# Seven half-size products for eight in two branch projections of a hybrid decoder layer

## The chip, the core and the metric

The kernel runs on one core of a Trainium2 chip. The core has five engines, each with its own instruction queue that it works off in order: TensorE (PE, matrix products; its weight loads, PEld, overlap them), VectorE (DVE), ScalarE (ACT), GpSimd (POOL) and SyncE (SP, which here only starts transfers). ACT and POOL start transfers too. Matrix products write to PSUM, which has eight banks of 128 x 512 floats; everything else lies in SBUF or, when it does not fit, in DRAM.

The metric is the time of one execution on the device, in microseconds (us); less is better. Before the change it is 1789.28 us, the median of three runs from 1788.69 to 1789.63.

## The reference

One layer of a decoder trunk, for 1024 positions of width 1024 (biases, lesser gains and the second half cut here):

```python
h = rms_norm(x, norm1_g)
proj = h @ w_in                          # all projections, the last 3 x 1024 columns are gate logits
p_rwkv, p_sb, q_mem, gate_logits = split(proj)
y_a = rwkv7_branch(p_rwkv)               # recurrence over positions, branch 0, width 512
y_b = stick_breaking_branch(p_sb)        # causal attention, branch 1, width 512
y_m = memory_branch(q_mem, mem)          # attention into 256 memory tokens, branch 2, width 512
ys = stack([y_a, y_b, y_m], axis=2)
branch_out = einsum('btnc,ncd->btnd', ys, w_branch)
merged = sum(sigmoid(gate_logits) * branch_out, axis=2)
x = x + merged @ w_out
x = x + conv_ffn(rms_norm(x, norm2_g))
```

The change concerns the products `ys[n] @ w_branch[n]` (1024 x 512 by 512 x 1024) of branches 1 and 2, and where the gates (`sigmoid`, 24 blocks of 128 columns by 1024 positions) are computed.

## The kernel before

**Precision.** Every product is made of three: both operands are split into a high part (an ACT copy that rounds, `split_raw`, L83) and a low part (the raw value less the high one, on POOL at L89 or DVE), and `mm3` (L107) adds high x high, high x low, low x high in one PSUM bank. So each operand costs one ACT and one POOL or DVE operation, and each block of the product three matmuls per 128 rows of depth and 512 columns.

**Items and filler.** The work that only fills PE is a list of generators (`items`, L1983 to L2007), and one step of a generator is six matmuls of 512 columns. `stream` starts each one an item ahead, which starts its weight load. `weave` (L1953) puts them between the steps of a main stream that is full of waits; a ratio says how many filler steps go to one step of the main stream.

**The main stream beside the change** is `stage2` (L601): the recurrence in 16 chunks of three steps. In step A PE applies the state, and DVE copies the result (L656); in step B PE solves within the chunk, and ACT copies the result (L664); in step C PE makes the output and the new state, which DVE adds to the old one (L674), while ACT copies the output (L676). The next A needs the new state, and the banks from which the output was copied. Between them `norm_part` (L693) takes the group norm of finished chunks: sums on DVE (L699), squares on ACT (L706, four of them a step), the square root on POOL (L195), the rescaling on DVE (L715). Then `group_norm` (L718) turns the result on PE, multiplies and adds on DVE (L729, L730) and splits it (L734, L735) for branch 0's product in `branch_last` (L1317), which follows at once.

**The filler beside it**, from the mark "y1" on: branch 1's products, the load and split of branch 2's input, branch 2's products with four of its gates between them, and the last two gates of branch 0. A branch is eight `branch_item`s (L1277), one for each 128 columns of output, of four steps each: with the split weight and the split input it fills two banks, and DVE multiplies them by the gate (L1297). For branch 2 POOL then adds branch 1's result, read back from DRAM (L1299), and POOL stores the sum in `mrd` (L1300). Gates are computed by `gate_item` (L879): eight steps, two ACT copies out of PSUM (L885), a rescaling on DVE by `rbc` (L886), a sigmoid on ACT (L889), and a store to `gsd`, from which the products load them (L1283). Four gates of branch 2 are not stored but kept.

**Buffers.** Gates and results use the three buffers of tag "w4"; raw weights two ("wr"), split weights two and two ("wh", "wl"). The normalised input x lies split in 16 tiles (xhi, xlo, eight each) until the last gate is done.

**Order.** Instructions marked by `pinned` (L124) stay in program order on their engine; while `strict` is set, as in this stretch, each one is also tied behind the pinned one before it. All others, DMAs among them, are placed by a planner.

Of the kernel before, what the change touches and what calls it, by code (L numbers as in the profile page):

```python
# [12 lines left out]
F32 = mybir.dt.float32  # L13
# [37 lines left out]
class Trunk:  # L51
# [11 lines left out]
    def t4(self, tag="w4", dt=F32, n=1024):  # L63
        pool = self.pool_a if tag in ("A", "it") else self.pool_w
        return pool.tile([128, n], dt, name=self.nm(tag), tag=tag, bufs=self.bufs_w[tag])

# [130 lines left out]
    def startup(self):  # L197
# [9 lines left out]
        self.xhi, self.xlo = ([self.pool_x.tile([128, 1024], F32R, name=f"x{n}{k}") for k in range(8)] for n in ("hi", "lo"))  # L207
# [112 lines left out]
    def row_norm(self, sq):  # L320
# [11 lines left out]
        self.rbc = self.pool_x.tile([128, 1024], F32, name="rbc")  # L332
# [920 lines left out]
    def load_y(self, b, st):  # L1253
        nc = self.nc
        ys, out = [], []
        st["y"] = out

        def first():
            for k in range(4):
                ys.append(self.t4("A", F32R))  # L1260
                nc.sync.dma_start(ys[k].bitcast(F32), self.yd[b, k])

        def split(k):
            if k == 0:
                st["hi"] = self.pool_a.tile([128, 4, 1024], F32R, name=self.nm("yhi"), tag="inst")
            hi, y = st["hi"][:, k], ys[k]
            self.pinned(nc.scalar.activation(hi, y.bitcast(F32), AF.Copy))
            self.pinned(nc.vector.tensor_tensor(y, y.bitcast(F32), hi.bitcast(F32), ALU.subtract))
            out.append((hi, y))

        return first, {3 + k: functools.partial(split, k) for k in range(4)}

# [4 lines left out]
    def branch_item(self, b, d, st, first):  # L1277
        nc = self.nc
        if d % 2 == 0:
            st["w", d // 2] = self.split_w(self.I["w_br"][b, d // 2])  # L1280
        if (b, d) in self.stored:
            st["g", d] = self.t4()
            nc.sync.dma_start(st["g", d], self.gsd[b, d])  # L1283
        if not first:
            o = self.t4()
            nc.sync.dma_start(o, self.mrd[d])
        yield
        pp = [self.ps("mm"), self.ps("mm")]
        for k in range(4):
            self.branch_mm(d, st["w", d // 2], st["y"], pp, k)  # L1290
            if k == 1:
                self.close_gates()
            yield
        g = st.pop(("g", d))
        for h in range(2):
            hs = slice(h * 512, (h + 1) * 512)
            self.pinned(nc.vector.tensor_tensor(g[:, hs], pp[h], g[:, hs], ALU.mult))  # L1297
        if not first:
            (nc.vector if d == 7 else nc.gpsimd).tensor_tensor(g, g, o, ALU.add)  # L1299
        nc.gpsimd.dma_start(self.mrd[d], g)  # L1300

    def branch(self, b, first):
        st = {}
        load, hooks = self.load_y(b, st)
        items = []
        for d in range(8):
            if (b, d) not in self.stored:
                items.append(self.gate_item(b, d, keep=st))
            items.append(self.branch_item(b, d, st, first))
        return load, items, hooks  # L1310
# [654 lines left out]
    def run(self):  # L1965
# [8 lines left out]
        self.stored, self.open_gates = set(), []  # L1974
# [17 lines left out]
        self.stored = set(gq)  # L1992
# [12 lines left out]
        ld1, br1, sp1 = self.branch(1, True)  # L2005
        ld2, br2, sp2 = self.branch(2, False)
# [34 lines left out]
        next(st2)  # L2041
        need("y1")
        self.strict = True
        self.weave(st2, pump, 2.08, 0)
        self.weave(self.group_norm(), pump, 1.0, 0)
        self.strict = False
        drain(pump)
# [80 lines left out]
```

## Time and profile before

| | |
|---|---|
| median of three runs | 1789.28 us |
| the profiled execution | 1788.33 us, its span 1786.6 us |
| PE busy | 1774.7 us, 99% |
| DVE, ACT, POOL busy | 1185.1, 883.3, 698.3 us |
| stage 2 in the span | 785.00 to about 981 us |
| group norm's turn and the last gate | about 981 to 1016 us |
| clock granted to PE | 1.00 |

The profile is of one execution. A row of a timeline gives start, length, engine, line, operation, output<-input and shape, and how often; in brackets the idle time of the engine before it and what ended it. A row of the groups gives line, engine, operation, tiles, shapes and count, then busy us and mean ns of one, then the idle time before them by what ended it. "x2" in a timeline row is two instructions merged.

### The profile page before, as it was taken

What the parts mean: (1) busy time and instruction counts of PE and PEld (TensorE: products, weight loads), DVE (VectorE), ACT (ScalarE), POOL (GpSimd) and SP (SyncE); (2) the same over time, 40 slices, a digit from 0 to 9 for tenths busy, and PEclk for the clock granted to TensorE, in tenths of its full rate; (3) what the DMA queues carried; (4) which work ended last, traced back from release to release, by engine and by line L of the source; (5) the groups of instructions that cost most, each with busy time, mean ns of one, the idle gap of its engine ahead of it and who ended that gap; (6) DMA issues with size and microseconds to landing.
All of it is one profiled execution on the core that took longest, in us unless ns stands there. A gap on an engine that the chain in (4) does not pass through costs nothing.

```text
span 1786.6 us, 27452 instructions
## 1 busy us (share of the span) xinstructions
PE 1774.7 (99%) x10481; PEld 1442.4 (81%) x10481; DVE 1185.1 (66%) x1687; ACT 883.3 (49%) x1667; POOL 698.3 (39%) x409
## 2 busy tenths in 40 slices
PE   9999999999999999999999999999999999999999
PEld 7777778878888888787777888887888888888887
DVE  5666674787888655243533873698767777795597
ACT  6544344566566635444546434454444445445343
POOL 1233252222231012122433321257777677535454
PEclk9999999999999999999999999999999999999999
DMA  4256574111112333658763653323323333396475
GB/s 185 74 166 193 181 244 148 51 57 42 54 57 77 103 126 93 203 181 278 269 228 145 230 211 105 108 89 124 101 89 104 115 104 113 109 329 224 142 246 202
DMA packets 120757, 263.39 MB, mean 147 GB/s; under 512 B 28329, under 2 KB 41129, under 8 KB 120498
## 3 DMA queue, kind: packets, MB, share of 16 engines
q1 hardware_dynamic: 82434, 193.31, 33.1%
q10 hardware_dynamic: 34416, 55.72, 8.5%
q0 software_dynamic: 3776, 12.62, 2.3%
q8 instruction: 82, 1.34, 0.3%
q14 instruction: 49, 0.40, 0.1%
HBM read 180.04 MB, written 81.53 MB: 146 GB/s over the span
## 4 chain that ended last, share of the span: by engine, by line
PE 61%; issue 1%; DVE 1%; POOL 1%; ACT 1%; DMA 1%; ACTq 0%; DVEq 0%; POOLq 0%; SPq 0%
PE mm L139 53%; PE g L139 8%; PE g L122 1%; POOL dw L1854 1%; DMA vmd<-w 0%; ACT wh L83 0%; DMA qk<-vd 0%; DVE qk L715 0%; ACT w L885 0%; DVE gall L1646 0%; DVE w L886 0%; DVE ga L1635 0%; DVE keep L1874 0%; DVE g L1629 0%; DVE g L1630 0%
## 5 line engine op out<-in xcount | busy, mean ns | idle before, releaser
L89 POOL TENSOR_TENSOR wl<-wr,wh 128x1024 fp32r<-128x1024 f32 x58 | 147.8, 2550 | 368.2 <-ACT wh L83 355.0
L139 PE MATMUL mm<-xhi,wh 128*128 128x512 f32 x784 | 260.5, 413 | 1.4 <-ACT xhi L222 1.0
L139 PE MATMUL mm<-xlo,wh 128*128 128x512 f32 x784 | 243.6, 392 | 0.1
L139 PE MATMUL mm<-xhi,wl 128*128 128x512 f32 x784 | 242.2, 390 | 0.0
L139 PEld LDWEIGHTS mm<-xlo,wh 128*128 128x128 f32 x784 | 147.0, 188 | 33.4 <-DVE xlo L225 1.0
L139 PEld LDWEIGHTS mm<-xhi,wl 128*128 128x128 f32 x784 | 147.2, 188 | 32.7
L139 PEld LDWEIGHTS mm<-xhi,wh 128*128 128x128 f32 x784 | 136.6, 189 | 31.1 <-issue 7.9
L139 PE MATMUL mm<-dw,da 128*128 128x512 f32 x528 | 120.9, 390 | 0.0
L83 ACT ACTIVATE wh<-wr 128x1024 fp32r<-128x1024 f32 x75 | 79.5, 1060 | 81.5 <-PE mm L139 57.2
L139 PE MATMUL mm<-BT,l 128*128 128x512 f32 x504 | 117.9, 389 | 0.3 <-POOL l L1555 0.3
L139 PEld LDWEIGHTS mm<-dw,da 128*128 128x128 f32 x528 | 98.9, 188 | 21.3 <-DVE da L1853 0.8
L1854 POOL TENSOR_TENSOR dw<-draw,dw 128x512 fp32r<-128x512 f32 x55 | 83.6, 1530 | 76.1 <-ACT dw L1852 74.2
L985 DVE TENSOR_TENSOR_SCAN at<-at,at 128x128 f32<-128x128 f32 (+3 forms) x64 | 91.0, 1428 | 33.1 <-ACT at L979 33.0
L139 PEld LDWEIGHTS mm<-BT,l 128*128 128x128 f32 x504 | 94.5, 188 | 20.3 <-POOL l L1555 0.7
L139 PE MATMUL mm<-BT,wh 128*128 128x512 f32 x352 | 108.6, 390 | 1.7 <-DVE u L1685 1.7
L139 PE MATMUL mm<-B,wh 128*128 128x512 f32 x352 | 108.6, 389 | 0.0
L195 POOL TENSOR_TENSOR hf<-rs,half 128x16 f32<-128x16 f32 (+1 forms) x18 | 49.2, 2734 | 142.2 <-DVE rs L192 137.8
L1853 DVE TENSOR_TENSOR da<-draw,da 128x512 fp32r<-128x512 f32 x77 | 66.9, 877 | 49.1 <-ACT da L1851 48.8
L139 PE MATMUL g<-dw,da 128*128 128x512 f32 x396 | 90.6, 389 | 0.4 <-POOL dw L1854 0.4
L1851 ACT ACTIVATE da<-draw 128x512 fp32r<-128x512 f32 x77 | 48.3, 628 | 80.7 <-PE mm L139 29.9
L139 PEld LDWEIGHTS g<-dw,da 128*128 128x128 f32 x396 | 74.2, 188 | 16.2 <-POOL dw L1854 0.8
L1555 POOL TENSOR_TENSOR l<-it,l 128x1024 fp32r<-128x1024 f32 x20 | 48.0, 2402 | 85.5 <-ACT l L1554 85.5
(343 smaller groups left out, 3972.1 us busy)
## 6 DMA issues: line engine op xcount, KB each, us to landing
wr<-in_w_in_dram SPq DMA_DIRECT2D x49, 512.0 KB, 3.7
draw<-actd SPq DMA_DIRECT2D x77, 256.0 KB, 3.3
at<-scr SPq DMA_DIRECT2D x28, 512.0 KB, 5.6
draw<-in_w_down_dram SPq DMA_DIRECT2D x55, 256.0 KB, 4.8
rw<-in_w_up_dram SPq DMA_DIRECT2D x22, 512.0 KB, 3.6
actd<-gall ACTq DMA_DIRECT2D x41, 256.0 KB, 3.4
gsd<-w ACTq DMA_DIRECT2D x20, 512.0 KB, 2.7
wr<-in_w_up_dram SPq DMA_DIRECT2D x18, 512.0 KB, 3.6
```

What stands on the lines that cost most here:

```text
L83: ins = self.nc.scalar.activation(hi, raw, AF.Copy)
L89: self.last_wl = self.nc.gpsimd.tensor_tensor(lo, raw, hi.bitcast(F32), ALU.subtract)
L122: self.pinned(self.nc.tensor.transpose(out, in_, self.ident[:n, :n]))
L139: self.pinned(self.nc.tensor.matmul(*a, **k))
L195: nc.gpsimd.tensor_tensor(out, t[:, :n], self.half[:, :n], ALU.pow)
L985: self.pinned(nc.vector.tensor_tensor_scan(sn[:, :W][:, ::-1], sn[:, :W][:, ::-1], self.smask[:, 1024 - W :][:, ::-1], 1.0, ALU.mult, ALU. ...
L1555: self.last_low = keep(eng.tensor_tensor(lo, src, hi.bitcast(F32), ALU.subtract))
L1851: self.pinned(nc.scalar.activation(A[:, 0], a, AF.Copy))
L1853: self.pinned(nc.vector.tensor_tensor(A[:, 1], a, A[:, 0].bitcast(F32), ALU.subtract))
L1854: nc.gpsimd.tensor_tensor(Wt[:, 1], w, Wt[:, 0].bitcast(F32), ALU.subtract)
```

## The change

Branches 1 and 2 are each computed in four groups n of 256 output columns (n = 0 to 3 for branch 1, 4 to 7 for branch 2). Input and weight of a group are cut in two by two blocks, and seven products of sums and differences of the blocks take the place of eight products of the blocks. Each of the seven is one filler step of six matmuls, so a group is seven steps where it was eight. The order is product 1 of group 0, and then 6, 2, 5, 7, 4, 1 of the next group, 3 of each group; the steps are counted s = 0 to 55.

- The input's operands (`operands`): four raw tiles are loaded, four differences made on DVE, and seven operands split (ACT, DVE). Branch 1's are made during the last two gates and steps 0 and 2; branch 2's are loaded at step 1 and made at steps 21 to 31.
- The weights (`weight_sums`, `weight`): sums on POOL, then an ACT copy and a POOL difference of 256 columns for each product, seven steps ahead.
- The results (`product`): PSUM banks A to D of a group are combined on DVE (one ACT copy) in halves of 512 columns and multiplied by the gate; `put` adds branch 1's result for n > 3 and stores.
- All 24 gates are computed ahead of both branches; all are stored and loaded again.
- x's 16 tiles become 16 buffers of one tag "xt", which the operands take over as the last gate releases them; `rbc` is taken over for partial sums.
- The ratio of filler to stage-2 steps goes from 2.08 to 1.92.

```diff
+    def xt(self, name, dt=F32R):
+        return self.pool_x.tile([128, 1024], dt, name=self.nm(name), tag="xt", bufs=16)
...
-    def load_y(self, b, st):
-    def branch_item(self, b, d, st, first):
-    def branch(self, b, first):
...
+    def branch_pairs(self):
...
+        N, L, R = 8, slice(0, 512), slice(512, 1024)
+        seq = [(0, 1)]
+        for n in range(N):
+            seq += [(n, 6), (n, 2), (n, 5), (n, 7), (n, 4)] + ([(n + 1, 1)] if n + 1 < N else []) + [(n, 3)]
...
+        def operands(b):
+            q11, q12, q21, q22 = raws[b]
...
+            def split(i, q, hi, lo):
+                act(hi, f(q), AF.Copy)
+                sub(lo, f(q), f(hi))
+                Y[b, i] = hi, lo
+
+            yield split(1, q11, big[0], big[1])
+            yield sub(q11, q12, q11)
+            yield split(2, q21, big[2], big[3])
+            t2 = st["t2"] = new(F32)
+            sub(t2, f(q22), q11)
+            yield sub(q21, t2, q21)
+            yield split(6, t2, new(), new())
+            yield split(5, q11, new(), new())
+            yield sub(q12, f(q22), q12)
+            yield split(7, q12, new(), low())
+            hi4, hi22 = new(), new()
+            yield split(4, q21, hi4, low())
+            yield split(3, q22, hi22, q22)
...
+        def weight_sums(n):
+            if n < N:
+                a11, a12, a21, a22 = quads(n)
...
+                gps(s1, a21, a22, ALU.add)
+                gps(s2, s1, a11, ALU.subtract)
+                gps(a21, a11, a21, ALU.subtract)
...
+        def weight(s):
...
+            if i == 3:
+                gps(a12, a12, S[n][1], ALU.subtract)
+            src = {1: a11, 2: a12, 3: a12, 4: a22, 5: S[n][0], 6: S[n][1], 7: a21}[i]
+            hi, lo = operand(s, wh), operand(s, wl)
+            act(hi, src, AF.Copy)
+            gps(lo, src, f(hi), ALU.subtract)
...
+        def gate(n, r):
+            if n < N:
+                g = G[n, r] = self.t4()
+                nc.sync.dma_start(g, self.gsd[1 + n // 4, n % 4 * 2 + r])
...
+        def put(n, r):
+            g, d = G.pop((n, r)), n % 4 * 2 + r
+            if n > 3:
+                (nc.vector if n == N - 1 else nc.gpsimd).tensor_tensor(g, g, st["o"][n % 2 * 2 + r], ALU.add)
+            nc.gpsimd.dma_start(self.mrd[d], g)
+
+        def product(s):
+            n, i = seq[s]
+            key, first = {1: ("A", True), 2: ("A", False), 6: ("B", True), 7: ("B", False), 5: ("C", True), 3: ("C", False), 4: ("D", True)}[i]
...
+            if i == 1:
+                act(p1, o, AF.Copy)
+            elif i == 6:
+                vec(x2, o, p1, ALU.add)
+            elif i == 5:
+                g = G[n, 0]
+                vec(g[:, L], bank.pop((n, "A")), g[:, L], ALU.mult)
+            elif i == 7:
+                vec(p1, o, p1, ALU.add)
+                vec(x3, bank[n, "C"], p1, ALU.add)
+            elif i == 4:
+                vec(p1, p1, o, ALU.subtract)
+                g = G[n, 1]
+                vec(g[:, L], p1, g[:, L], ALU.mult)
+                vec(g[:, R], x3, g[:, R], ALU.mult)
+                put(n, 1)
+                gate(n + 1, 0)
+                old(n + 2, 1)
+            elif i == 3:
+                vec(x2, o, x2, ALU.add)
+                g = G[n, 0]
+                vec(g[:, R], x2, g[:, R], ALU.mult)
+                put(n, 0)
+                gate(n + 2, 1)
+                old(n + 2, 0)
+
+        def run():
...
+            for s in range(len(seq)):
+                product(s)
+                n, i = seq[s]
+                weight(s + 7)
+                if s == 0:
+                    self.close_gates()
+                    gate(1, 1)
+                if s % 7 == 1:
+                    load_w(s // 7 + 2)
+                if s % 7 == 5:
+                    weight_sums(s // 7 + 2)
+                if s in (0, 2):
+                    next(st["y"])
+                if s == 1:
+                    load_y(2, [self.xt("q", dt) for dt in (F32, F32, F32, F32R)])
+                elif s == 20:
+                    st["y"] = operands(2)
+                elif 21 <= s <= 31 and s != 27:
+                    next(st["y"])
...
+        hooks1 = {1: begin, 3: step, 5: step}
+        hooks2 = {0: hook(w_first, lambda: tiles(F32, F32R)), 1: hook(step, w_next, lambda: tiles(F32R, F32R)), 2: hook(step, lambda: tiles(F32R, F32R)),
+                  3: hook(step, lambda: tiles(F32R, F32R)), 4: sums_first, 5: hook(step, weights(0, 1)), 6: hook(step, weights(2, 3)), 7: lambda: weight_sums(1)}
...
-        items += [lambda: drain(inv), ld1, gate(sp1), gate(), gate(), mark("y1"), *br1, ld2, gate(sp2), *br2, gate(), gate()]
+        load1, hooks1, hooks2, pairs = self.branch_pairs()
+        items += [lambda: drain(inv), load1, gate(), gate(), gate(), mark("y1"), *[gate() for _ in range(5)], gate(hooks1), gate(hooks2), pairs]
...
-        self.weave(st2, pump, 2.08, 0)
+        self.weave(st2, pump, 1.92, 0)
```

131 lines of the change are left out of this document (81 added, 50 removed).

## The prediction

> **What bounds the kernel now.** First the head of the page, then its stretches, then the instructions in order of time where the change lands.
>
> ```profile
> span 1786.6 us, 27452 instructions
> ...
> PE 1774.7 (99%) x10481; PEld 1442.4 (81%) x10481; DVE 1185.1 (66%) x1687; ACT 883.3 (49%) x1667; POOL 698.3 (39%) x409
> ```
>
> TensorE (PE) is the bound: 12 us of idle in the span. The windows view of the stretch that changes (columns: stretch, its length, then busy us and instructions of PE, PEld, DVE, ACT, POOL; clock; DMA share; GB/s) says the same, and what stands behind it:
>
> ```profile
> 840.00:860.00 20.00, 20.00 (x234) 15.78 (x233) 9.17 (x23) 17.52 (x59) 6.70 (x4) 1.00 0.98 374
> ...
> 940.00:960.00 20.00, 20.00 (x232) 15.75 (x232) 6.16 (x20) 15.50 (x61) 10.61 (x5) 1.00 0.47 166
> 980.00:1000.00 20.00, 20.00 (x116) 16.72 (x112) 14.86 (x33) 10.45 (x33) 7.42 (x4) 1.00 0.51 181
> 1000.00:1020.00 20.00, 20.00 (x98) 16.49 (x97) 17.25 (x22) 10.53 (x15) 8.14 (x4) 1.00 0.69 243
> 1020.00:1040.00 20.00, 20.00 (x90) 16.58 (x89) 18.54 (x27) 9.95 (x17) 10.02 (x4) 1.00 0.83 296
> 780.00:980.00 200.00, 199.28 (x2071) 156.47 (x2069) 81.73 (x237) 106.10 (x393) 64.66 (x38) 1.00 0.66 227
> ```
>
> From 780 to 980 PE idles 0.7 us, at clock 1.00, and DVE and ACT have room on average. Not everywhere: ACT is at 17.5 of 20 in one slice, DVE at 15 to 18.5 from 980 on. This is where stage 2 (the RWKV recurrence, 16 chunks of three steps A, B, C) is woven with products that only fill PE. One chunk in order of time:
>
> ```profile
> 785.00 0.68 PE L139 MATMUL g<-qk,at 64*64 64x64 f32 x16
> 785.41 0.62 DVE L656 COPY ys<-g 128x64 f32<-128x64 f32 x4
> ...
> 788.56 0.68 PE L139 MATMUL g<-ys,qk 64*64 64x64 f32 x16
> 788.94 1.86 ACT L664 ACTIVATE qk<-g 64x64 f32<-64x64 f32 x8 [2.48 <-PE g L139]
> ...
> 792.12 1.15 PE L139 MATMUL g<-qk,at 128*64 128x64 f32 x32
> 792.70 0.97 DVE L674 SCALAR_TENSOR_TENSOR ys<-ys,pc,g 128x64 f32<-128x64 f32 x4 [5.48 <-PE g L139]
> 793.01 1.87 ACT L676 ACTIVATE qk<-g 64x64 f32<-64x64 f32 x8
> ...
> 971.91 0.57 PE L139 MATMUL g<-ys,at 64*64 64x64 f32 x12
> ```
>
> Each step's result must pass DVE or ACT before the next step on PE: DVE has 788.56 - 786.03 = 2.5 us to spare after A, ACT 792.12 - 790.80 = 1.3 us after B. Both queues keep program order here, so whatever is put ahead of these copies eats that margin, and PE, in order too, then stands. That is the measure for the change.
>
> **What PE saves.** The filler's pitch, from one branch product:
>
> ```profile
> 779.92 0.62 PE L139 MATMUL mm<-A,wh 128*128 128x512 f32 x2
> ...
> 784.46 0.61 PE L139 MATMUL mm<-yhi,wl 128*128 128x512 f32 x2
> ```
>
> 20 matmuls start between these rows: 4.54/20 = 0.227 us each, 1.365 us for a filler step of six. Before, two branches took 2 x 8 x 4 = 64 steps; now 8 groups of 7 products are 56. Gate steps are as many as before. Gain: 48 x 0.227 = 10.9 us. Stage 2's own part stays: 15 chunks from 785.00 to 971.91 are 12.46 us each, less 6.24 fillers x 1.365 leaves 1.31 us a step. The ratio 1.92 for 2.08 spends the eight steps fewer evenly; about four of 50 stage-2 steps get one filler instead of two, which B's 1.3 us margin covers to within 0.1: nothing.
>
> **What ACT and DVE get.** Their prices:
>
> ```profile
> L1297 DVE TENSOR_TENSOR w<-mm,w 128x512 f32<-128x512 f32 x32 | 20.5, 683 | 17.9 <-PE mm L139 13.6 <-DMA w<-gsd 4.3
> ...
> L886 DVE TENSOR_TENSOR w<-w,rbc 128x1024 f32<-128x1024 f32 x6 | 14.9, 2482 | 15.5 <-ACT w L885 15.5
> ...
> L83 ACT ACTIVATE wh<-wr 128x1024 fp32r<-128x1024 f32 x14 | 14.8, 1055 | 14.3 <-issue 13.2 <-POOL hf L195 1.0
> ...
> L885 ACT ACTIVATE w<-mm 128x512 f32<-128x512 f32 x12 | 6.5, 593 | 0.1
> ...
> L1299 DVE TENSOR_TENSOR w<-w,w 128x1024 f32<-128x1024 f32 x1 | 1.2, 1216 | 0.0
> ```
> ```profile
> 779.69 2.35 DVE L1268 TENSOR_TENSOR A<-A,yhi 128x1024 fp32r<-128x1024 f32 x2
> ...
> 785.94 1.28 DVE L1297 TENSOR_TENSOR w<-mm,w 128x512 f32<-128x512 f32 x2
> ```
>
> Back to back a DVE operation of 512 columns takes 0.64 us and of 1024 1.18. An ACT split of 256 columns is not in the trace; between 64 columns (0.22, the copies above), 512 (0.59) and 1024 (1.06) I estimate 0.42. A group of seven drains with 9 DVE operations where a pair of products had 4; each branch needs 7 splits and 4 differences of 1024 columns where it had 4 splits. Averaged over the stretch DVE gets 40 x 0.64 + 14 x 1.18 = 42 us more on 82 of 200: room enough. So it is decided at the places where they bunch; there are three.
>
> **Entry** (last gate, from its second step, to product 0; 8 fillers, four stage-2 steps: 8 x 1.365 + 4 x 1.31 = 16.2 us of PE). The group norm's squares fall here, four a step:
>
> ```profile
> 845.05 0.34 ACT L706 ACTIVATE jk<-qk,hn 128x64 f32<-128x64 f32 x1
> ...
> 846.80 1.04 ACT L1267 ACTIVATE yhi<-A 128x1024 fp32r<-128x1024 f32 x1
> ```
>
> Four squares and their sums take 1.75. ACT: 16 of these 7.0, two sets of stage-2 copies 3.7, splits of operands 6, 5, 7, 4 at 1.05 = 4.2, eight weight splits 3.4, the gate's two drains 1.2, two sigmoids 2.1, product 1's copy 0.6: 22.2, 6 more than PE's time. Less the 1.3 margin PE waits 4.7; I take 4.5. Ends: 0.5 if the splits, which need only loaded data, slip into earlier idle time; 6 if no margin is left.
>
> **Middle** (products 20 to 31, where branch 2's operands are made; 12 x 1.365 + 6.25 x 1.31 = 24.6 us). The norm's second burst lies here:
>
> ```profile
> 936.28 1.39 DVE L699 TENSOR_REDUCE hn<-qk 128x4 f32<-128x256 f32 x4
> ...
> 958.83 3.65 DVE L715 TENSOR_SCALAR qk<-qk,hn,hf 128x64 f32<-128x64 f32 x16
> 962.40 0.85 DVE L699 TENSOR_REDUCE hn<-qk 128x2 f32<-128x128 f32 x4
> ```
> ```profile
> 963.63 0.72 PE L139 MATMUL g<-ys,qk 64*64 64x64 f32 x16 [0.44 <-DVE ys L656]
> ```
>
> In the kernel before this burst alone already stopped PE, by 0.44. DVE after: 13 drains x 0.64 = 8.3, 11 splits and differences x 1.18 = 13.0, two chunks of stage 2 at 0.62 + 0.97 = 3.2, the norm 3.65 + 1.39 + 0.85 + 0.5 = 6.4: 30.9, 6.3 too many; less the 2.5 margin 3.8. To this comes POOL, which now cuts every operand's low half, 11 operations of 256 columns a group:
>
> ```profile
> 980.33 2.40 POOL L89 TENSOR_TENSOR wl<-wr,wh 128x1024 fp32r<-128x1024 f32 x1 [9.18 <-ACT wh L83]
> ```
> ```profile
> 981.46 2.35 DVE L886 TENSOR_TENSOR w<-w,rbc 128x1024 f32<-128x1024 f32 x1 [8.08 <-ACT w L885]
> ```
>
> A DVE operation that reads two SBUF tiles while POOL runs ends with POOL's: L886 has a mean of 2482 ns in this stretch against 1216 for the same shape (L1299 on DVE). L1297, which reads PSUM, stays near 683. POOL's 256 columns are not in the trace; a quarter of 2.4 is 0.6, with a start-up I estimate 0.73. It is then busy 12 x 11/7 x 0.73 = 13.8 of 24.6 us; 15 two-SBUF operations (11 and four gate products) meet it 56% of the time halfway: 15 x 0.56 x 0.37 = 3.1. Middle: 6.9; ends 2 (half the excess hidden in idle time before) and 11 (each meets it at its start). The Trainium skill (SBUF — State Buffer, "Who interferes with whom") says that such a pair is an exclusive lock and that the loser waits for the whole instruction. The rows above agree; without that rule the sum would be 3.1 lower, a result within no change.
>
> **End** (products 40 to 55 beside the group norm's turn; then branch 0's product needs its output at once):
>
> ```profile
> 1011.11 2.57 DVE L735 TENSOR_TENSOR A<-qk,qk 128x512 fp32r<-128x512 f32 x1
> ...
> 1014.98 0.69 DVE L735 TENSOR_TENSOR A<-qk,qk 128x512 fp32r<-128x512 f32 x1 [0.70 <-ACT qk L734]
> ```
> ```profile
> 1016.34 1.09 PE L139 MATMUL mm<-A,wh 128*128 128x512 f32 x4
> ```
>
> The last low half ended at 1015.67 and PE read it at 1016.34: 0.7 us to spare. From 980 to 1020 DVE was busy 14.9 + 17.3 = 32.1 of 40. Out go two gate rescales at 2.5 and one product's drain and add, 1.3 + 1.2: 7.5. In come 23 drains x 0.64 and two adds x 1.2: 17.1. That is 41.7 in 40. If all 7.9 us of idle can be filled, PE waits 9.6 - 7.9 - 0.7 = 1; if none, 9. I take the middle, 5.
>
> **The gate's way round.** Three w4 buffers hold gates. A group's odd gate goes to DRAM after its product 4, and only then can the next group's even gate be loaded, wanted five products later (the second read by DVE, with stage 2 queued behind it):
>
> ```profile
> L1300 POOL DMA_DIRECT2D mrd<-w x16: 531/572/616, 787.5 to 997.8; - x16
> ...
> DMA to landing us min/median/max: 2.9/5.8/7.9
> ```
> ```profile
> L1283 SPq DMA_DIRECT2D w<-gsd x12: 319/319/320, 765.8 to 887.1; - x12
> ...
> DMA to landing us min/median/max: 3.3/4.1/4.8
> ```
>
> Three drains 2.0 + store 5.8 + load 4.1 = 11.9 against 5 x 1.365 + 2.6 x 1.31 = 10.2: 1.7 late, inside DVE's 2.5. I take 0.5; with the longest landings 14.7, 2 beyond the margin in each of three groups, 6. SP waits with the load, and stage 2's own loads stand behind it; these are due a chunk later. Four more gates are stored and loaded, 4 MB at the window's 227 GB/s, off the path. In groups 4 to 6 POOL's add (2.4) lengthens the way round, but stage 2 has ended by then or is about to.
>
> **Costed at nothing.** Branch 2's gates move ahead of both branches with their weight loads, splits, rescales and sigmoids: the same steps, and stage 2 runs beside them as it did beside products. The operands' tiles come free as the last gate's steps finish, two a step, each at least three steps before the product that reads it. Branch 0's first weight split waits for the products up to 51 to leave its buffer, four products or some 6 us ahead of its use; without that lead it would be the 1.06 of the split and POOL's 2.4.
>
> **Sum.** -10.9 + 4.5 + 6.9 + 5 + 0.5 = +6.0 on the profiled execution's 1788.33: 1794.3. The median of the runs shown, 1789.28, stands 0.95 above that execution, so 1795 for the runs.
>
> **Rivals.**
> - *The queues absorb it; PE keeps its gain.* For: DVE has 59% and ACT 47% idle from 780 to 980, and operand work needs only loaded data. Against: program order, and 1.3 and 2.5 us of margin. Faster: with the low ends 0.5 + 2 + 1 and no gate wait, 1789 - 10.9 + 3.5 = 1782. It decides if ACT and DVE start the operands' work so early that no burst costs over 7 us in all. Chance 0.25.
> - *One or two bursts spill.* 1789 - 10.9 + 7 to 14: 1785 to 1792, about the time of before. Chance 0.25.
> - *The gate's way round becomes the loop.* Stores land at 7 to 8 us as beside stage 2's loads, and DVE stops in every group: 6 on the forecast, 1801; with POOL's lock at its high end 1805. Chance 0.15.
>
> **How the numbers follow.** The forecast, all three bursts (1792 to 1799), has 0.35. The range 1781 to 1806 leaves the gain without any wait (1778) and all high ends together below 2 in 10. A measurement tells 0.2%, 3.6 us, from no change: faster is the first rival and a little of the second, 0.27; same 0.22; slower 0.51.
>
> **What would show it.** Right: 48 matmuls fewer; PE idle by 13 to 20 us in three places, ended by ACT L664 (stage 2's copies) at the entry, DVE L656 or L674 in the middle, and at the end by the low halves of L735; DVE and ACT near 20 of 20 there. Wrong: PE full through these stretches; or a wait of DVE for the gate's load; or a wait for a weight's low half on POOL, which I cost at nothing because weights are cut seven products ahead (about 13 us, against some 8 of POOL's work in a group).

## The result, and the profile after

The changed kernel takes 1858.68 us (median of five runs, 1858.22 to 1859.65), beside 1789.28 for the kernel before: ratio 1.0388, interval 1.0373 to 1.0403. It is slower by 69.4 us where 5.7 were forecast, and lies outside the range of 1781 to 1806. The profiled execution took 1859.65 us. Line numbers below are those of the changed kernel, three higher than before up to the branch part (L667, L679, L659, L718 were L664, L676, L656, L715); L1262, L1263 and L1264 record the ACT, DVE and POOL work of the new part but for the adds (L1372); its stores are L1373, its loads of gates and of branch 1's results L1363 and L1367.

The head of its page:

```profile
span 1857.9 us, 27591 instructions
...
PE 1792.9 (97%) x10433; PEld 1451.0 (78%) x10433; DVE 1255.9 (68%) x1742; ACT 902.7 (49%) x1729; POOL 748.8 (40%) x488
...
PEclk9999999999999999999888889999999999999999
```

Two things have changed. PE idles 1857.9 - 1792.9 = 65.0 us, where it idled 11.9: 53.1 more. And PE is busy 18.2 us longer although it runs 48 matmuls fewer (10433 for 10481), which should have taken 10.9 off: 29.1 us are a slower pitch of the same work. 53.1 + 29.1 - 10.9 = 71.3 is the difference of the spans. The row of the granted clock says where: five slices, some 880 to 1110 us, the stretch of the change. By windows (columns as in the prediction):

```profile
900.00:920.00 20.00, 12.69 (x104) 9.77 (x105) 6.69 (x15) 10.27 (x34) 11.41 (x12) 0.74 0.67 229
940.00:960.00 20.00, 14.43 (x140) 10.96 (x138) 12.30 (x27) 9.07 (x38) 8.43 (x12) 0.83 0.74 263
980.00:1000.00 20.00, 11.46 (x76) 8.35 (x76) 16.22 (x39) 7.99 (x27) 9.11 (x11) 0.74 0.63 216
...
1040.00:1060.00 20.00, 12.31 (x52) 9.75 (x51) 19.55 (x21) 3.79 (x9) 18.69 (x16) 0.83 0.56 184
1060.00:1080.00 20.00, 9.72 (x33) 7.23 (x32) 18.34 (x18) 4.94 (x7) 10.27 (x9) 0.76 0.73 285
```

Before, the prediction's rows have PE at 199.28 of 200 from 780 to 980 and at 20.00 in each slice from there to 1040, all at clock 1.00. Now up to half of a slice is lost, and only from 1040 on is DVE full. So up to 1000 no engine is full on average, and the question is who waits for whom. The instructions in order of time show it, first at the entry:

```profile
898.02 1.72 POOL L1264 TENSOR_TENSOR s<-wr 128x256 f32<-128x256 f32 x1
899.45 0.57 ACT L1262 ACTIVATE t<-mm 128x512 f32<-128x512 f32 x1
903.25 0.72 POOL L1264 TENSOR_TENSOR wr<-wr,s 128x256 f32<-128x256 f32 x1
904.00 0.42 ACT L1262 ACTIVATE wh<-wr 128x256 fp32r<-128x256 f32 x1 [3.98 <-POOL wr L1264]
908.48 1.61 ACT L667 ACTIVATE qk<-g 64x64 f32<-64x64 f32 x7
908.97 1.89 PE L142 MATMUL g<-ys,at 64*64 64x64 f32 x16 [7.23 <-ACT qk L667]
...
912.69 1.22 PE L142 MATMUL mm<-y,wh 128*128 128x512 f32 x2
```

Weight 3 of a group is a difference that POOL makes (`wr<-wr,s`) just before ACT can split it. It stands in POOL's queue behind three sums and three low halves, comes at 903.25, and ACT, which has nothing else it may do in its order, stands from 900.02 to 904.00 with a sigmoid, an operand's split, squares and stage 2's copy (L667) queued behind it. PE waits 7.2 us for that copy. The row of 912.69 shows the second loss: two matmuls take 1.22 us where the prediction's rows have 0.62, half the pitch, at a granted clock of 0.50; this lasts until about 916.3.

Middle:

```profile
938.95 4.92 DVE L718 TENSOR_SCALAR qk<-qk,hn,hf 128x64 f32<-128x64 f32 x8
945.49 0.57 POOL L1373 DMA_DIRECT2D mrd<-w  x1 [1.90 <-DVE ys L677]
946.08 0.74 POOL L1264 TENSOR_TENSOR wr<-wr,s 128x256 f32<-128x256 f32 x1
946.85 0.42 ACT L1262 ACTIVATE wh<-wr 128x256 fp32r<-128x256 f32 x1 [8.35 <-POOL wr L1264]
947.79 1.42 PE L142 MATMUL g<-ys,at 64*64 64x64 f32 x12 [5.57 <-ACT qk L679]
...
986.31 4.97 DVE L718 TENSOR_SCALAR qk<-qk,hn,hf 128x64 f32<-128x64 f32 x16
992.17 0.61 DVE L659 COPY ys<-g 128x64 f32<-128x64 f32 x4
992.44 0.80 PE L142 MATMUL g<-ys,qk 64*64 64x64 f32 x10 [6.33 <-DVE ys L659]
```

A ring of all three engines: DVE is held in the norm's rescaling (4.92 us while POOL runs), POOL's store of a result waits for DVE, the difference for weight 3 stands behind the store, ACT's split waits for it, stage 2's copy stands behind that, PE waits. At 986 DVE itself stops PE, by 6.3 us, in the burst that was forecast; its longest row is again the norm's rescaling, 4.97 us for sixteen instructions where the prediction's row has 3.65.

End:

```profile
1040.06 3.35 POOL L1372 TENSOR_TENSOR w<-w,y 128x1024 f32<-128x1024 f32 x1 [3.92 <-DVE w L1263]
1041.11 4.71 DVE L718 TENSOR_SCALAR qk<-qk,hn,hf 128x64 f32<-128x64 f32 x4
1049.29 0.68 DVE L1263 TENSOR_TENSOR rbc<-mm,t 128x512 f32<-128x512 f32 x1
1050.03 1.22 PE L142 MATMUL mm<-y,wh 128*128 128x512 f32 x2 [7.69 <-DVE rbc L1263]
...
1061.01 5.38 DVE L733 TENSOR_TENSOR qk<-at,at 128x512 f32<-128x512 f32 x1
1061.42 0.75 POOL L1264 TENSOR_TENSOR wl<-wr,wh 128x256 fp32r<-128x256 f32 x1
1062.12 0.74 POOL L1264 TENSOR_TENSOR wr<-wr,s 128x256 f32<-128x256 f32 x1
1062.82 2.34 POOL L1372 TENSOR_TENSOR w<-w,q 128x1024 f32<-128x1024 f32 x1
1065.11 0.72 POOL L1264 TENSOR_TENSOR wl<-wr,wh 128x256 fp32r<-128x256 f32 x1
1067.69 0.68 DVE L1263 TENSOR_TENSOR rbc<-mm,rbc 128x512 f32<-128x512 f32 x1
1068.43 1.22 PE L142 MATMUL mm<-y,wh 128*128 128x512 f32 x2 [5.29 <-DVE rbc L1263]
```

A bank takes two products, and DVE reads it between them (`product`: x2 after 6, x3 after 7). PE may go on in that bank only when DVE has read it, and DVE's read stands behind the group norm's turn (L733, L738, L718), several steps of which are slow while POOL runs: one operation of 0.7 us takes 5.38 while POOL goes through four instructions. In the two rows of PE product 7 waits for x2; at 1035 and 1079 product 3 waits for x3, 2.6 and 5.0 us. Between the middle and the end, at 1021, PE waits 6.2 us more for stage 2's copy (L667), which stands behind the split of a weight 3 as at the entry.

A last pair of rows, from the queue of SP and from DVE, answers the prediction's question about the gate's load:

```profile
998.90 18.36 SPq L1367 DMA_DIRECT2D q<-mrd  x4
...
1022.01 0.69 DVE L1263 TENSOR_TENSOR w<-mm,w 128x512 f32<-128x512 f32 x1 [7.68 <-DMA w<-gsd]
```

SP stands 18 us in the loads of branch 1's results and issues the next gate's load only behind them, at 1017.79.

### The profile page after: what moved, and what is told of

Read it like the earlier page. It is cut to its first block, busy times and chain, and to the rows that moved or that the text cites. A ratio compares the mean times of both kernels' runs of the same rounds, so it can differ in the third digit from the quotient of the medians.

```text
span 1857.9 us, 27591 instructions
## 1 busy us (share of the span) xinstructions
PE 1792.9 (97%) x10433; PEld 1451.0 (78%) x10433; DVE 1255.9 (68%) x1742; ACT 902.7 (49%) x1729; POOL 748.8 (40%) x488
## 4 chain that ended last, share of the span: by engine, by line
PE 53%; DVE 5%; issue 3%; POOL 3%; ACT 3%; DMA 1%; SPq 0%; ACTq 0%; DVEq 0%; POOLq 0%
PE mm L142 45%; PE g L142 7%; POOL dw L2001 1%; PE g L125 1%; DVE qk L718 1%; POOL wl L1264 1%; DVE qk L733 1%; DVE w L1263 1%; DVE rbc L1263 0%; ACT jk L709 0%; POOL wr L1264 0%; DVE da L2000 0%; POOL w L1372 0%; DMA vmd<-w 0%; ACT qk L679 0%
## 5 line engine op out<-in xcount | busy, mean ns | idle before, releaser
L92 POOL TENSOR_TENSOR wl<-wr,wh 128x1024 fp32r<-128x1024 f32 x50 | 126.9, 2539 | 350.3 <-ACT wh L86 350.2
L86 ACT ACTIVATE wh<-wr 128x1024 fp32r<-128x1024 f32 x67 | 71.1, 1061 | 80.2 <-PE mm L142 74.0
L889 DVE TENSOR_TENSOR w<-w,rbc 128x1024 f32<-128x1024 f32 x24 | 41.3, 1722 | 61.0 <-ACT w L888 58.7
```

The costliest lines, as they stand in the source:

```text
L86: ins = self.nc.scalar.activation(hi, raw, AF.Copy)
L92: self.last_wl = self.nc.gpsimd.tensor_tensor(lo, raw, hi.bitcast(F32), ALU.subtract)
L889: self.last(nc.vector.tensor_tensor(g, g, self.rbc, ALU.mult))
```

## The experiments

Differences are medians against 1858.68 unless another kernel is named. The ratios to the kernel before have intervals of some 0.003 to each side, 5 us, so a difference of less than 5 us between two of these kernels is not settled. The theories: A, in-order waits over POOL and ACT for the weights (C: for the gate's load); B, DVE's own work; M, banks read between their products; K, stalls that lower PE's clock. A band is the range that a theory gave before the run.

**e1, the difference for weight 3 taken early** (with weight 2, five products before its split):

```diff
-            if i == 3:
-                gps(a12, a12, S[n][1], ALU.subtract)
-            src = {1: a11, 2: a12, 3: a12, 4: a22, 5: S[n][0], 6: S[n][1], 7: a21}[i]
+            src = {1: a11, 2: a12, 3: S[n][1], 4: a22, 5: S[n][0], 6: S[n][1], 7: a21}[i]
...
             gps(lo, src, f(hi), ALU.subtract)
+            if i == 2:
+                gps(S[n][1], a12, S[n][1], ALU.subtract)
```

> The difference that weight 3 needs (on POOL) is made five products earlier, written over a sum that is used up by then; nothing else changes and nothing is left out. Theory A (chain): POOL makes this difference in the queue behind the group's store, which waits for DVE; ACT's split of weight 3 waits for it (58.3 us in 8 waits in the changed kernel), stage 2's copies wait behind on ACT, PE behind them. Then those waits fall below 15 us and the time falls by 20 to 45 us, to 1815 to 1840. Theory B (the prediction's: PE waits because operand splits and drains bunch on ACT and DVE): the time stays within 6 us of 1859.

1848.18, 10.5 less; in neither band. ACT's waits for POOL's sums and differences fall from 58.3 us to 11.3 (in the view of waits, 760 to 1100 us), and PE's wait at the entry falls to 3.14. But what was queued behind now waits for DVE:

```profile
904.76 1.43 PE L142 MATMUL g<-ys,at 64*64 64x64 f32 x12 [3.14 <-ACT qk L667]
...
1023.46 0.68 DVE L1263 TENSOR_TENSOR t<-mm,rbc 128x512 f32<-128x512 f32 x1
1024.19 0.79 PE L142 MATMUL mm<-y,wh 128*128 128x512 f32 x1 [9.59 <-DVE t L1263]
```

The coupling is real and worth 10 of 69 when it is removed alone; a stall of 9.6 us stands where two of 6.2 and 2.6 stood.

**e2, the results stored from SP's queue:**

```diff
-            nc.gpsimd.dma_start(self.mrd[d], g)
+            nc.sync.dma_start(self.mrd[d], g)
```

> The groups' results are stored from SP and no longer from POOL; nothing is left out. Theory A: in groups 0 to 3, which have no add, POOL no longer stands for DVE before the difference, so half of ACT's waits for POOL go, and the time falls by 10 to 25 us; in groups 4 to 6 the add on POOL still stands there. Theory B: within 6 us of 1859. Theory C (the gate's way round: store, load, multiply): the store lands sooner, and DVE's wait for a gate's load (7.7 us, once) goes; the time falls by 5 to 10 us.

1854.13, 4.5 less: inside B's band, below A's and C's least, and too little to be settled. The stall at 947 falls from 5.6 to 2.1 us as the ring above says; others grow, from 2.6 to 5.9 us at 1031 and from 5.0 to 9.3 at 1073. DVE's wait of 7.7 us for a gate's load goes, as C says, but one of 5.4 us comes at 931.

**e5, e1 with every `put`, its gate's load and the old result's load issued two products later:**

```diff
-                put(n, 1)
-                gate(n + 1, 0)
-                old(n + 2, 1)
+                later(s, lambda: (put(n, 1), gate(n + 1, 0), old(n + 2, 1)))
```

> The difference for weight 3 is taken early, as in e1_diff_early, and every result is added, stored and followed by its gate's load two products later in program order, so that POOL's store no longer holds up the weights behind it while DVE is late. If in-order waiting in POOL's queue is what costs (theory A), the two together give more than the 10.5 us and 4.5 us of e1 and e2: 1825 to 1842. If the work itself, on POOL and DVE beside the group norm, is the limit (theory B), the order changes little: 1844 to 1852.

1850.89: no better than e1 alone, and in B's band. So the place of POOL's stores in the order is not what e1 leaves.

**e3, branch 2's operands not made** (its products read the raw loads; 11 DVE and 7 ACT operations left out):

```diff
-                    st["y"] = operands(2)
-                elif 21 <= s <= 31 and s != 27:
-                    next(st["y"])
+                    next(operands(2), None)
...
+                for i in range(1, 8):
+                    Y[2, i] = raws[2][i % 4], raws[2][i % 4]
```

> Branch 2's operands are not made: its products read the raw loads, so 11 DVE operations and 7 ACT splits of 1024 columns are left out at products 21 to 31, and the output differs. Theory B: the middle loses its burst, the time falls by 7 to 20 us. Theory A: the waits of ACT for POOL stay in all groups; the time falls by no more than 8 us.

1852.02, 6.7 less, just short of B's band and inside A's, with the DVE stall at 992 down from 6.3 to 4.5 us. That is the size which the prediction gave to its middle burst, but it is not the whole burst: with no operand made at all, the norm's rescaling takes longer than before, while POOL goes through five instructions from 981.19 to 984.9, and PE waits 4.5 us behind it:

```profile
980.17 6.76 DVE L718 TENSOR_SCALAR qk<-qk,hn,hf 128x64 f32<-128x64 f32 x16
```

**e6, no low halves of the weights** (left out; products read the high half), **e7, no adds** (branch 1's result neither loaded again nor added), **e8, both:**

```diff
-            gps(lo, src, f(hi), ALU.subtract)
...
-                    self.mmul(o, operand(s, (wh, wl)[u], k), y[v][:, k], start=(first and k == 0 and pi == 0),
+                    self.mmul(o, operand(s, (wh, wh)[u], k), y[v][:, k], start=(first and k == 0 and pi == 0),
```
```diff
-            if n < N and "o" in st:
+            if False:
...
-            if n > 3:
-                (nc.vector if n == N - 1 else nc.gpsimd).tensor_tensor(g, g, st["o"][n % 2 * 2 + r], ALU.add)
```

> POOL makes no low halves of the weights; the products read the high half in their place (output differs). 56 instructions of 0.73 us, 41 us of POOL's work, are gone; sums, differences, adds and stores stay. Theory A (what is queued on POOL is late, and ACT's copy of weight 3 and DVE's two-tile instructions with it): two thirds of the loss go, 1800 to 1820. Theory B (DVE's own work beside the group norm): 1840 to 1855.

> Branch 1's result is neither loaded again nor added for n over 3 (output differs): six POOL adds of 2.4 to 3.4 us, two on DVE and eight loads are gone, all after 980 us. Theory A, POOL's long adds starving DVE at the end: the stalls after 1000 us fall by half, 1825 to 1840. Theory C, SP waiting at the first of those loads ahead of a gate's: the stall at 1021 us alone goes, 1848 to 1853. Theory B: 1850 to 1859.

> Both: no low halves and no adds (output differs). POOL then has only sums, differences and stores. Theory A: nearly all of the loss goes and the 48 matmuls show, 1785 to 1800 (by the 7.5 us that the gates cost in e4, 1786 at the least). Theory B: the DVE bursts at 990 and after 1040 stay, 1825 to 1845.

1848.44, 1847.35 and 1836.30: 10.2, 11.3 and 22.4 less. e6 and e8 lie in B's bands, e7 in none, just below C's. The two add up, but POOL without this work gives back a third of the loss, not all. In e7 the stall at 1021 falls from 6.2 to 2.0, so POOL's adds, standing ahead of weight 3's difference, made most of it (e7 also leaves out the loads for them; e14 below speaks against these). With POOL relieved DVE still keeps PE waiting 6.6 us at the end of e8:

```profile
1053.82 0.69 DVE L1263 TENSOR_TENSOR t<-mm,rbc 128x512 f32<-128x512 f32 x1
1054.66 0.77 PE L142 MATMUL mm<-y,wh 128*128 128x512 f32 x1 [6.64 <-DVE t L1263]
```

**e9, five of DVE's nine operations a group left out** (each bank read once, by the gate's product):

```diff
             elif i == 6:
-                vec(x2, o, p1, ALU.add)
...
             elif i == 7:
-                vec(p1, o, p1, ALU.add)
-                vec(x3, bank[n, "C"], p1, ALU.add)
...
-                vec(p1, p1, o, ALU.subtract)
...
-                vec(g[:, R], x3, g[:, R], ALU.mult)
+                vec(g[:, R], bank[n, "C"], g[:, R], ALU.mult)
...
-                vec(x2, o, x2, ALU.add)
```

> DVE does not form the combinations of a group's products (five of its nine operations of 0.6 us a group are left out, 40 in all, 24 us of DVE); each bank is read once, multiplied by the gate (output differs). POOL's work and ACT's are as in the changed kernel. If DVE's share of the products is what cannot be hidden (theory B), most of the loss goes: 1800 to 1825, the stalls after 1000 us first. If the weights' chain over POOL and ACT is (theory A), 1845 to 1856: the stalls of 5 to 7 us at 909, 948 and 1021 stay.

1843.73, 15.0 less for 40 operations (DVE's busy time falls by 39.0 us, from 1255.9 to 1216.9): the largest single part, and still under a quarter; below A's band and above B's. The stalls at 909 and 1011 stay (7.2 and 5.4), as A says, but that at 948 falls to 2.8, against A; the stalls of the end, from 1025 on, fall from 20.6 to 15.3 us together, and at 1062 one of 7.6 is left.

**e10, all of this left out at once** (the edits of e3, e6, e7 and e9, and ACT's copy of product 1):

```diff
-            if i == 1:
-                act(p1, o, AF.Copy)
```

> All side work out at once: no low halves of the weights, no operands of branch 2, no adds, no combinations, no drain of the first product on ACT (output differs). What stays is the 48 matmuls fewer, the order of products, gates ahead, and the loads and stores. If the side work is the whole cause, the time is that of before less 10.9 plus the 7.5 of the gates' place: 1783 to 1790. If the order of the products itself (one bank each, free two products later, where the kernel before had two pairs) starves PE, 1800 to 1830.

1814.74, 43.9 less, in the band of the products' order and not in that of side work alone. The parts alone give 10.2 + 11.3 + 6.7 + 15.0 = 43.2, so within what is settled they add up. But 25 us above the kernel before remain with almost no side work:

```profile
PE 1779.7 (98%) x10433; PEld 1442.3 (79%) x10433; DVE 1186.4 (65%) x1689; ACT 893.3 (49%) x1714; POOL 688.3 (38%) x426
...
1007.46 12.71 PE L142 MATMUL mm<-q,wh 128*128 128x512 f32 x47 [5.58 <-DVE w L1263]
1035.81 1.62 PE L142 MATMUL mm<-q,wh 128*128 128x512 f32 x3 [6.73 <-DVE w L1263]
```

DVE's busy time is back at that of before (1185.1), and PE still waits for it.

**e13 and e14, no loads of the gates** (DVE multiplies by a resident constant), in e10 and in the changed kernel, here the first of four products of each:

```diff
-                nc.sync.dma_start(g, self.gsd[1 + n // 4, n % 4 * 2 + r])
...
-                vec(g[:, L], bank.pop((n, "A")), g[:, L], ALU.mult)
+                vec(g[:, L], bank.pop((n, "A")), self.kon[:, :512], ALU.mult)
```

> As e10_bare, and the gates of the branches are not loaded: DVE multiplies by a resident constant (output differs), so that nothing waits for store, load and buffer. If the gate's way round over DRAM makes the two stalls of 5.6 and 6.7 us that e10 has at its end (theory C), they go with the slow matmuls behind them: 1792 to 1800. If the order of products with single banks makes them, 1810 to 1816.

> The changed kernel with all its side work, without the loads of the gates (multiplied by a resident constant; output differs). Theory C: the gate's load costs what it costs in e10, 10 to 20: 1839 to 1849. If it is hidden behind the other waits as long as these stand, 1853 to 1860.

1812.20 (2.5 less than e10) and 1854.92 (3.8 less): the gate's way round is hidden for the most part; both times lie in the bands against C, and both differences are too small to be settled. In e14 PE's stall at 1021 stays (6.25 us at 1020), so SP's 18 us did not make it. What makes the last one of e13:

```profile
1022.73 2.90 DVE L738 TENSOR_TENSOR A<-qk,qk 128x512 fp32r<-128x512 f32 x1
...
1026.16 2.59 DVE L738 TENSOR_TENSOR A<-qk,qk 128x512 fp32r<-128x512 f32 x1
1028.67 0.68 DVE L1263 TENSOR_TENSOR w<-mm,kon 128x512 f32<-128x512 f32 x1
...
1031.25 1.28 DVE L1263 TENSOR_TENSOR w<-mm,kon 128x512 f32<-128x512 f32 x2
...
1032.68 2.90 PE L142 MATMUL mm<-q,wh 128*128 128x512 f32 x6 [6.72 <-DVE w L1263]
```

The reads of banks stand behind the group norm's turn; PE goes on when the last of them, in the row of 1031.25, is done. The same turn ran in the kernel before, beside a gate:

```profile
987.11 0.71 PE L139 MATMUL mm<-xhi,wh 128*128 128x512 f32 x2
...
1001.25 0.62 PE L139 MATMUL mm<-xhi,wl 128*128 128x512 f32 x2
```

There PE runs products of x (48 matmuls, 10.9 us, in two banks) for which it needs nothing from DVE. All gates are now ahead, and the norm stands beside products that need DVE every two or three.

**e17 and e18, no bank read:** in e13 and in the changed kernel each operand from a bank is replaced by a resident constant, with the same number of operations, as here in e18:

```diff
-                vec(x2, o, p1, ALU.add)
+                vec(x2, self.kon[:, :512], p1, ALU.add)
```

> As e13_bare_no_gate, but DVE's four operations of a group read a resident constant twice, never a product's bank, so that PE gets each bank back from itself (output differs). Theory M: the stalls of 3.2 us at 1004 and 6.7 us at 1033 and the slow matmuls behind them go, 12 to 18 of the time: 1794 to 1801. If the end's stalls come from elsewhere, 1808 to 1816.

> The changed kernel with all its side work and the same number of operations on DVE and ACT, but a constant in place of each bank that they read (output differs). Theory M: the stalls after 1030 us (2.6, 7.7, 5.3 and 5.0) go with the slow matmuls behind them, some 20 + 12; the stalls of stage 2's own steps before that stay: 1822 to 1832. If what costs at the end is not the banks, 1845 to 1860.

e17: 1804.21, 8.0 less than e13; both stalls are gone, as M says, but the time stays 3 above its band, and a new one of 4.9 us stands at 1009. The substitution has a part in that: DVE's operations now read SBUF twice and hold up POOL's difference for weight 3:

```profile
1005.20 3.30 POOL L1264 TENSOR_TENSOR wr<-wr,s 128x256 f32<-128x256 f32 x1
1005.43 2.48 DVE L1263 TENSOR_TENSOR w<-kon 128x512 f32<-128x512 f32 x4
1009.00 1.22 PE L142 MATMUL mm<-q,wh 128*128 128x512 f32 x2 [4.88 <-ACT wh L1262]
```

e18: 1862.91, not faster, against M's forecast and 3 above the other band. The waits of PE for DVE's reads are gone there too, and in their place PE waits for weights' low halves on POOL (5.47 us at 1045, 3.36 at 1069). As the constants also load POOL's side, this does not show what the banks alone are worth in the full kernel; it shows that the next waits stand right behind.

**e11, a bank more** (from group 5 on bank D from the other four) **and e12, the group norm spread** over more products:

```diff
-                bank[n, key] = self.ps("mm")
+                bank[n, key] = self.ps("g" if key == "D" and n > 4 else "mm")
```
```diff
-        self.weave(st2, pump, 1.92, 0)
-        self.weave(self.group_norm(), pump, 1.0, 0)
+        self.weave(st2, pump, 1.75, 0)
+        self.weave(self.group_norm(), pump, 1.5, 0)
```

> From group 5 on the fourth product's bank comes from the other four banks, so that a bank of the first three is wanted again one product later. If the few banks make each late read of DVE a stall (theory M, margin), the stalls after 1030 us (5.3 to 7.7 us three times) shrink by about 1.4 us each and the time by 4 to 10: 1849 to 1855. If DVE is simply full there (theory B), 1856 to 1861.

> The group norm begins earlier against the products and takes 1.5 products a step for 1 (stage 2 has 1.75 a step for 1.92). If the density of DVE's work beside the group norm is the cause of the end's part (theory B), the stalls after 1030 us fall by half: 1835 to 1848. If stage 2 with fewer products a step loses as much as the end gains, 1850 to 1862; if the end is not about the group norm at all, more.

1859.60 and 1856.46: nothing, each in the band against its theory. In e11 the stalls are the same to 0.03 us (2.64, 7.67, 5.29, 5.01): PE does not wait for a free bank but to go on in one that DVE has still to read. In e12 the stalls move and keep their sum.

**e4, the kernel before with branch 2's last four gates ahead of both branches**, stored and loaded again:

```diff
-        gq[14:14] = [(2, d) for d in range(4)]
+        gq[14:14] = [(2, d) for d in range(8)]
...
-        items += [lambda: drain(inv), ld1, gate(sp1), gate(), gate(), mark("y1"), *br1, ld2, gate(sp2), *br2, gate(), gate()]
+        items += [lambda: drain(inv), ld1, gate(sp1), gate(), gate(), mark("y1"), *[gate() for _ in range(4)], *br1, ld2, gate(sp2), *br2, gate(), gate()]
```

> The kernel before, with only the four gates of branch 2 moved ahead of both branches, stored and loaded again; eight products as before. If the loss lies in the seven products (theories A, B and C) this stays within 4 us of 1789.3. If it lies in the gates' place (stage 2 beside other filler, four more stores and loads) it is slower by over 10 us.

1797.09, ratio 1.0052 (1.0033 to 1.0071): 7.5 us slower than its runs of before, between the two bands, with PE's idle up from 11.9 to 16.9. So moving these four gates alone costs, with the old products. Branch 0's last two gates, which stood beside the group norm's turn, stay there in e4; the change moves them too, and no run tries that by itself.

**e15 and e16, stalls by themselves:** the kernel before, with a low half repeated on DVE in the last phase, where PE is otherwise full: 28 times at one step in e15, as here, and 16 times at steps 38, 49, 60 and 71 in e16.

```diff
-            self.pinned(nc.vector.tensor_tensor(A[:, 1], a, A[:, 0].bitcast(F32), ALU.subtract))
+            for _ in range(28 if s in (60,) else 1):
+                self.pinned(nc.vector.tensor_tensor(A[:, 1], a, A[:, 0].bitcast(F32), ALU.subtract))
```

> The kernel before, with 27 extra repetitions of one low half on DVE (0.6 us each) in the last phase, where PE is full and its operands are cut some 8 us ahead: one stall of PE of about 9 us. If a stall by itself lowers the granted clock (theory K), the time rises by the stall and 3 to 5 us more: 1801 to 1804. If the low clock belongs to the change's place and not to stalls, by the stall alone: 1797 to 1799.

> The same with 15 repetitions at four places: four stalls of about 2 us. If only long stalls lower the clock, the time rises by the sum of the stalls, 8: 1796 to 1798. If every stall does, by 3 to 5 more each: 1808 to 1818.

DVE has less to spare there than I took, so the stalls came out longer: one of 17.4 us, and four of 7.8 to 10.7 (35.4 together). The times are 1810.63 and 1834.70, 21.0 and 45.1 more than before. PE's busy time, for the same matmuls, rises by 1778.1 - 1774.7 = 3.4 us in e15 and 10.8 in e16. The windows of e15 behind its stall and later, and three windows of one us of e16 behind its first stall (from its first, fifth and sixth us):

```profile
1755.00:1761.00 6.00, 5.76 (x17) 4.59 (x18) 5.93 (x9) 1.45 (x3) 1.54 (x1) 0.65 0.43 134
1767.00:1773.00 6.00, 6.00 (x28) 4.95 (x27) 5.32 (x5) 4.25 (x8) 4.61 (x4) 1.00 0.97 343
```
```profile
1684.84:1685.84 1.00, 1.00 (x2) 0.83 (x3) 1.00 (x2) 0.00 (x0) 0.00 (x0) 0.50 0.12 10
...
1688.84:1689.84 1.00, 1.00 (x5) 0.84 (x4) 0.00 (x0) 0.43 (x1) 0.00 (x0) 0.90 0.95 336
1689.84:1690.84 1.00, 1.00 (x6) 0.80 (x5) 0.69 (x1) 0.72 (x2) 0.20 (x1) 1.00 1.04 393
```

Right behind its stall e15 runs 17 matmuls in 6 us at a mean granted clock of 0.65, and 28 in the same time later. Taken in windows of one us the clock is 0.50 for the first 4.0 to 4.6 us behind each of the five stalls of e15 and e16, and 1.00 after that. Nothing of the change is in these kernels, so K holds for stalls of 8 to 17 us: each costs itself and, by PE's busy time, 2.7 to 3.4 us more. They do not show stalls of 2 us, but other traces do, and not all alike: in the changed kernel the clock falls to 0.50 about 1.1 us behind the stalls of 2.6 us at 970 and 1035, for some 3.4 us, and in e4 right behind that of 2.9 us, but not behind e4's other two, of 1.4 and 1.7, nor behind one of 2.6 us in e7 (at 1031). So a short stall can lower the clock; what decides it was not found. The Trainium skill (TensorE: Matmul & The Clock Gate, "Part 1: The HAM clock gate") says that PE's clock is halved after idling and given back after some 3.4 us of work; the rows agree with the half, and the return came somewhat later, after 4.0 to 4.6 us behind these five stalls.

No version of the seven products came near the kernel before: with nearly all of its side work left out e17 still takes 14 us more than its runs of before.

## Why the prediction was wrong

In its own steps:

- *PE's gain, 10.9.* Right in the matmuls (x10433); the time shows nowhere, as the clock takes it back.
- *Entry, 4.5 (0.5 to 6).* Place and releaser (L667) as named; 7.2 us of idle, above the range. Four of them ACT spent waiting for POOL, which the step did not have. With the difference early (e1) 3.1 remain, inside the step's range; whether ACT's load makes them, as the step says, no run singles out.
- *Middle, 6.9 (2 to 11).* DVE's stalls there are 2.6 + 6.3, and e3 measures 6.7 for the operands. That the two numbers agree is partly luck: without the operands 4.5 us of stall stay, behind L718, which the step did not count among the operations that POOL holds up; its sixteen instructions went from 3.65 to 4.97 us, and in e3 to 6.76. The 5.6 at 947 came over POOL and ACT and was not foreseen. A POOL instruction of 256 columns took 0.73, as estimated, but a DVE operation was not held up by half of one: it lost to runs of them (5.38 above). The step also read its rows loosely: DVE's operation does not end with POOL's, which ended at 980.33 + 2.40 = 982.73, but 1.08 us later, about its own length.
- *End, 5 (1 to 9).* Mis-sized by far: 2.6 + 7.7 + 5.3 + 5.0 = 20.6 us of idle, ended by DVE's reads of banks and not by the low halves that the step named. The step compared DVE's work with the length of the stretch, as though PE could run ahead. It cannot: the bank is read between its two products. Fewer operations on DVE (e9) bring the idle of the end down to 15.3 us, and no adds (e7) to 16.5; the rest of what e9 and e7 give falls elsewhere.
- *The gate's way round, 0.5 (0 to 6).* DVE waits 7.7 us for a load, but without loads the time falls by 3.8 (e14) or 2.5 (e13): within the range; the wait of DVE that was to show a wrong forecast is there, and the third rival, which made a loop of it, did not happen.
- *Costed at nothing.* This failed first. Weights cut "seven products ahead" are ahead only if POOL's queue is: e1 gives 10.5, e6 10.2, and the 6.2 us of PE at 1021 come the same way. And gates moved ahead were "the same steps"; what they took along was the cover of the group norm's turn and of branch 2's operands. e4 puts 7.5 on the move of four gates with the old products; e13 shows the turn uncovered, but what the two gates that stood beside it would be worth was not measured.
- *Not in the sum: the clock.* 29.1 of the 71.3 us, over nine stalls of 2.6 us and more 3.2 us each. Three stalls foreseen would have had some 9 us added.

The prediction's waits come to 16.9 us; PE's idle rose by 53.1. Its direction was right, with the places of its stalls, but only in part for its reasons; its first rival (queues absorb it) was further off. Most of the error goes back to two assumptions: that in-order queues delay only their own work, and that an idle microsecond of PE costs a microsecond.

What is accounted for, from 1858.7 down: side work 43.9 (e10), gates' loads 2.5 (e13), banks read between products 8.0 (e17), which leaves 1804.2. Against 1789.3 - 10.9 = 1778.4 some 26 stay. In e17 these are 13.7 of idle (3.2 at the entry, 4.9 for a weight, the rest small) and 12.0 of slow pitch. How much of them is the gates' place, how much weight 3's difference and how much the order of the products was not separated.

## What to carry to other kernels

A filler is worth what PE can do with it without asking another engine: 48 matmuls into two banks cover a burst of 10 us, a product whose bank is read before its second half covers 3, so count matmuls for each read, and look which burst the moved filler was covering. In queues that keep program order follow each small new instruction to what stands behind it on its engine, over all engines, before it is costed at nothing. Add to each forecast stall of several microseconds the slow matmuls behind it, here about 3 us each.

## What was unexpected of the hardware

- After a stall PE runs at half pitch: 1.22 us for two matmuls of 512 columns instead of 0.62, granted clock 0.50 for 4.0 to 4.6 us behind stalls of 8 to 17 us, and 2.7 to 3.4 us more of PE's busy time for each. Stalls of 2.6 to 2.9 us lowered it too, in the changed kernel twice and in e4 once, but in e7 one did not.
- A DVE operation with two SBUF operands can lose to several POOL instructions in a row, not to one: 5.38 us for 0.7 us of work. The Trainium skill (SBUF — State Buffer, "Who interferes with whom") has the loser wait for the whole instruction; here it lost to four in a row.
- DVE's rescaling by a scalar from a tile (L718, four operations) went from 0.98 to 4.71 us while POOL ran an add, a low half and a sum (1040.06 to 1045.76), though it has one wide operand. The same section lists this form among those that can contend with POOL; the prediction had counted only operations on two tiles.
